# A TensorE-bound transformer step: the low parts of the attention keys on both halves of the partitions

## The chip, the cores and the metric

One core of a Trainium2 chip. The metric is the device time of one execution in microseconds (us); less is better.

## The reference

One inference step of a two-layer backbone, for 128 context tokens and 512 latent tokens, 1024 features, all in float32. Each layer: modulation, one input projection for four mixers (attention, spatial gating, retention, pooling), an output projection with residual and layer norm, and a gated convolutional feed-forward part. The change lies in the attention. It has two key heads (kv) with two query heads each (g), 64 features a head. Context queries see the context keys; the queries of a latent block of 128 see their own block, its neighbours within a window, and 128 cached keys. The two kinds share one softmax, with a sink logit beside them:

```python
s_loc = jnp.einsum("bnqkgd,bnjkd->bnkgqj", qb, kw).astype(F32) * scale
s_loc = jnp.where(valid[None, :, None, None], s_loc, NEG_INF)
s_ctx = jnp.einsum("bnqkgd,bjkd->bnkgqj", qb, ck).astype(F32) * scale
p = softmax_with_sink(jnp.concatenate([s_loc, s_ctx], axis=-1), sink).astype(v.dtype)
```

## The kernel before

Five token tiles of 128 (t = 0 is the context, 1 to 4 the latent blocks) run through both layers; weights stream from DRAM. A float32 product is made of rounded parts: an operand is split into a high part (float32r) and a low part, the rest, and high x high, high x low and low x high are summed in PSUM. For weights, ScalarE makes the high part (L245) and VectorE the low part by a subtraction (L246). The projections (fm_mms, L547 to L549, and tm_mm, L819 to L821) take these three products for each of eight row blocks of 128; a unit of 128 output features goes first over the tokens 0 to 383 (384 columns), then over 384 to 639 (256 columns).

The order of work is the order of the program's text: each engine runs its instructions in that order. `mixers` writes projections in line and weaves "lanes" between them: after each half projection `tick` runs one stage of every open lane. The attention blocks are such lanes; t = 1, 3, 0 run in one, t = 2, 4 in a second. GpSimd's affine steps of the layer before (`affine`, L503 and L504) and the retention setup (L661) are woven in by the same ticks.

The keys are 64 features a head, so head 0 lies on partitions 0 to 63 and head 1 on 64 to 127. `key_split` (L573 to L579) makes, for each head, a high part that ScalarE writes to both halves of the partitions (L578), and a low part that VectorE writes in place (L579), one tile for both heads. It runs twice a layer: on the cached keys in `attn_setup2` (128 columns, tile ckh) and on the projected, rotated keys in `mixers` (640 columns, tiles kh and kl, L1104 and L1105). `query_split` (L582 to L589) builds, for a block, queries with the high part on the head's own half (L587, ScalarE) and the low part on the other half (L588, VectorE). So one 128-row product of such a query tile with the doubled high keys sums high x high and low x high. A second product, of 64 rows, adds high x low. That is the pair in `attn_block`:

```python
T.matmul(o, z[:, h, :], kh[kv][:, cols], start=True, stop=False)
T.matmul(o, z[r0:r0 + HD, h, :], kl[r0:r0 + HD, cols], start=False, stop=True,
         tile_position=(r0, 0))
```

A block makes two stages of scores, one for each key head, each with both of its query heads; a stage is called a group below. Blocks 1 and 4 have two key blocks (256 columns) and the cached keys (128 columns), blocks 2 and 3 three key blocks (384) and the cached keys, block 0 only its own 128. Then VectorE adds the mask and takes the maximum (L766; L763 for block 0), ScalarE takes the exponential (L780), VectorE scales (L785), TensorE transposes the probabilities (L794), they are copied to SBUF (L798, L800), and TensorE multiplies with the values (L809).

Work tiles of up to 664 columns come from one pool of 25 buffers (`unit`): keys, split keys, queries, probabilities, weights' helpers. In `mixers` the split of the 640 keys stands behind the last key projection; the first query split of block 1 follows it after one more half projection (384 columns) and the copies of it.

Of the kernel before, what the change touches and what calls it, by code (L numbers as in the profile page):

```python
# [8 lines left out]
F32 = mybir.dt.float32  # L9
F32R = mybir.dt.float32r  # L10
# [4 lines left out]
P = 128  # L15
D = 1024
KD = D // P
# [72 lines left out]
def kernel(  # L90
# [38 lines left out]

    # ---- persistent tiles  # L130
    ident = one.tile([P, P], F32, name="ident")
# [18 lines left out]

    # ---- weight stream: stages in the order of their use, split ahead of it
    class Cols:
# [36 lines left out]
    class AdaFirst:  # L189
        """128 rows of the adaLN columns that the first projection waits for, used as they come"""  # L190

# [19 lines left out]
    class AdaPair:  # L211
        """a sixth of the columns and two steps for later use, in a unit's place; each step has rows of its own"""
        n = 1
# [35 lines left out]
    class Stream:  # L249
# [20 lines left out]
        def advance(self, limit=99):  # L270
            """emit splits, in stream order, while there is room for them"""
            while self.there and limit > 0 and self.live < NW // 2:
                st = self.there[0]
                self.count += not isinstance(st, AdaPair)
                eng = G if self.pool_share and self.count % self.pool_share == 0 else V
                got = st.fetch() if isinstance(st, AdaPair) else split(*st.view(self.u_split), eng)
                self.ready.append((st, got))
                self.live += 1
                limit -= 1
                self.u_split += 1  # L280
                if self.u_split == st.n:
                    self.there.pop(0)
                    self.u_split = 0
                    if not isinstance(st, AdaPair):
                        self.dma()
# [6 lines left out]
        def take(self):  # L292
            """the next unit of a projection; adaLN products before it are made on the way"""
            st, w = self.head()
            while isinstance(st, AdaPair):
                st.step(w)
                self.free()
                st, w = self.head()
            return w
# [6 lines left out]

    # ---- adaLN: rows of products in PSUM, then feature-major columns and gate rows
    class Ada:
# [31 lines left out]
    def ada_finish(a, ss):  # L340
        """columns of the features, or rows of a gate"""
        f = folds[len(ss) - 1]
        if ss[0] in (2, 5):
            pg = bank(name="adaG")
            T.matmul(pg[0:4, :], f, row, start=True, stop=True)
            gr = unit([P, 512], name="grow")
            S.activation(out=gr[0:4, :], in_=pg[0:4, :], func=AF.Copy)
            for j in range(2):
                side(out=a.scratch[ss[0] // 3, :, j * 512:(j + 1) * 512], in_=gr[2 * j:2 * j + 2, :])
            return  # L350
        n = 4 * len(ss)
        pt = bank(4 * n, name="adaT")
        for q in range(4):
            T.matmul(pt[:, q * n:(q + 1) * n], row[:, q * P:(q + 1) * P], f, start=True, stop=True)
        ptv = pt.rearrange("p (q j c) -> p q j c", q=4, c=2)
        for i, s in enumerate(ss):
            for j in range(2):
                V.tensor_copy(out=a.modT[:, s if s < 2 else s - 1, 4 * j:4 * j + 4, :], in_=ptv[:, :, 2 * i + j, :])
# [8 lines left out]

    # ---- per-layer small parameters, feature major
    def params(l, dma):
# [25 lines left out]
    def mods(a, prm_ln, which):  # L395
        """scale and bias columns [P, KD, 2] of the modulated activation"""
        sh, sc = a.modT[:, 2 * which], a.modT[:, 2 * which + 1]
# [17 lines left out]

    # ---- residual stream: alpha * x in token-major halves, kept in DRAM between uses
    xs = {}
# [51 lines left out]
    def norm_out(t, lnwb, dst):  # L469
        """the first half on VectorE, the second on ScalarE and GpSimd (and VectorE in the end)"""  # L470
        lw, lb = lnwb
# [34 lines left out]

    # ---- normalized token-major tile -> modulated, split, feature-major h
    def to_h(t, sb):
# [24 lines left out]

    # ---- feature-major projection of one 128-column unit onto tokens lo:hi
    GA, GB = (0, SPLIT_COL), (SPLIT_COL, W)

    def fm_mms(us, lo, hi, lag=0, mid=None):
        """several units side by side, each lag steps behind the one before"""
        pss = [bank(hi - lo, name="fm") for _ in us]
# [14 lines left out]

    # ================= mixers =================
    class Mix:
# [16 lines left out]
    def key_split(k, kh, kl):  # L573
        """keys of both heads: the high part of each on both halves of the partitions, the low parts in place"""
        for kv in range(2):
            r = slice(kv * HD, kv * HD + HD)
            for j in range(2):
                S.activation(out=kh[kv][j * HD:j * HD + HD, :], in_=k[r, :], func=AF.Copy)  # L578
            V.tensor_tensor(out=kl[r, :], in0=k[r, :], in1=kh[kv].bitcast(F32)[r, :], op=ALU.subtract)  # L579

    def query_split(m, c0):
        """queries of each head with the low part on the other half of the partitions"""  # L582
        z = unit([P, 4, P], name="qs").bitcast(F32R)
        for kv in range(2):
            r, o = slice(kv * HD, kv * HD + HD), slice(HD - kv * HD, P - kv * HD)
            q, zz = y8[r, 0:2, c0:c0 + P], z[:, 2 * kv:2 * kv + 2, :]
            S.activation(out=zz[r], in_=q, func=AF.Copy)  # L587
            V.tensor_tensor(out=zz[o], in0=q, in1=zz.bitcast(F32)[r], op=ALU.subtract)  # L588
        return z  # L589

    def attn_setup2(m):
        pt = bank(P, name="ckT")
        T.transpose(pt, m.ck, ident)
        u = unit([P, 3, P], name="ckh").bitcast(F32R)
        m.ckh, m.ckl = [u[:, 0, :], u[:, 1, :]], u[:, 2, :]
        key_split(pt, m.ckh, m.ckl)
# [7 lines left out]
    def decays():  # L604
        """log decays of every layer"""
        n = DEPTH * 8
        dec = small(n, "dec")
        side(out=dec, in_=ret_decay.rearrange("l a h -> (l a h)").partition_broadcast(P))
        # log_sigmoid(x) = min(x, 0) - 2 atanh(t / (2 + t)), t = exp(-|x|)
        ab = small(n, "ab")  # L610
# [22 lines left out]
    def states():  # L633
        """initial latent states"""
        for l in range(DEPTH):
# [3 lines left out]
    def centre():  # L639
        """over the value dimension"""  # L640
        n = DEPTH * 4
# [58 lines left out]

    # ---- attention
    SWAP = [(i + 16) % 32 for i in range(32)]
# [23 lines left out]
    def attn_block(m, t, first=False):  # L726
# [16 lines left out]
        for kv in range(2):  # L743
            r0 = kv * HD
            for g in range(2):
# [3 lines left out]
                while i < nb:  # L749
                    kind, bt = blocks[i]  # L750
                    w = 1
                    while kind == "k" and i + w < nb and blocks[i + w] == ("k", bt + w):
# [4 lines left out]
                    T.matmul(o, z[:, h, :], kh[kv][:, cols], start=True, stop=False)  # L757
                    T.matmul(o, z[r0:r0 + HD, h, :], kl[r0:r0 + HD, cols], start=False, stop=True,  # L758
                             tile_position=(r0, 0))
                    i += w  # L760
# [51 lines left out]

    # ---- token-major values
    def tm_mm(t, units):
# [40 lines left out]

    # ---- spatial gating: s = ws v + bs, feature major
    def sgu(m):
# [15 lines left out]

    # ---- retention
    def ret_step(m, d, t, kv, s1=None):
# [8 lines left out]
    def ret_states(m, l):  # L884
        """k^T v of every chunk and the states that enter the chunks"""
        kvp = {}
# [99 lines left out]

    # ---- multiscale pooling
    def pool_in(ps_a, ps_b):
# [44 lines left out]

    # ---- lanes: chains of stages that are woven between the projections
    lanes, late = [], []
# [21 lines left out]
    def mixers(l, m, prm, mid=None, then=None):  # L1057
# [45 lines left out]
        m.k = raws[2]  # L1103
        m.kh, m.kl = [unit([P, W], name="kh").bitcast(F32R) for _ in range(2)], unit([P, W], name="kl").bitcast(F32R)  # L1104
        key_split(m.k, m.kh, m.kl)  # L1105
# [96 lines left out]

    # ---- FFN depthwise conv
    def conv_a(cwT, f, ps):
# [22 lines left out]

    # ================= the stream of weights =================
    def wout_chunk(l, k, h):
# [41 lines left out]

    # ================= program =================
    def x_in(t):
# [16 lines left out]
    def h_first(segs, alone=0):  # L1290
        """modulated, split h from the feature-major x in y8"""
        lo, hi = segs[0][1], segs[-1][2]
# [57 lines left out]
    for l in range(DEPTH):  # L1350
# [4 lines left out]

        # output projection, residual, layer norm
        xd = drm.tile([NT, P, D], F32, tag="xd", name=nm("xd"))
# [38 lines left out]

        # gated conv FFN
        act, outs, queue = [], {}, []
# [25 lines left out]
        for i, (br, f) in enumerate(order):  # L1424
# [7 lines left out]
            while len(queue) > (4 if i < 5 else 2):  # L1432
                finish_b(queue.pop(0))
        # the last groups leave the first columns of hh and hl to the products that follow
        EARLY = 4
# [129 lines left out]
```

## Time and profile before

| | |
|---|---|
| median of three runs | 1594.93 us (1594.81 to 1595.16) |
| span of the profiled execution | 1593.2 us |
| TensorE matmul busy | 1558.6 us, 98% of the span |
| VectorE, ScalarE, GpSimd busy | 953.3, 617.9, 420.9 us |
| mean granted TensorE clock | 0.992 of full speed |

The profiled execution has no time of its own beside its span; the span, from the first to the last instruction, is 1.7 us under the median of the runs, and what lies around it is taken as the same before and after. In the profile PE is TensorE, PEld its weight load, DVE VectorE, ACT ScalarE, POOL GpSimd, SP SyncE; L758 is line 758 of the kernel. Matmuls overlap: the distance from one start to the next says what a matmul costs, its own duration does not.

### The profile page before, as it was taken

Reading aid. Unit: us, or ns where it says so; the run is one execution under the profiler, and the core shown is the slowest. Engines: PE = TensorE matmul, PEld = TensorE weight load, DVE = VectorE, ACT = ScalarE, POOL = GpSimd, SP = SyncE. Lnnn points to the kernel's source line nnn. Section 1 sums busy time; section 2 is a strip of 40 time slices with the busy share of each in tenths; the row PEclk is TensorE's granted clock in tenths of the full one; section 3 lists DMA queues with packets and bytes.
Section 4 is the critical chain, followed back from the end, with each engine's and each line's share of the span. In section 5 each row is a group of like instructions: output and inputs, shape, how many; then the busy total and the mean of one; then the engine's idle time right before and its main releaser. Section 6 shows DMA issues by size and latency. Waiting matters only on the chain.

```text
span 1593.2 us, 24481 instructions
## 1 busy us (share of the span) xinstructions
PE 1558.6 (98%) x9708; PEld 1360.9 (85%) x9708; DVE 953.3 (60%) x1856; ACT 617.9 (39%) x994; POOL 420.9 (26%) x486
## 2 busy tenths in 40 slices
PE   5999999999999999999998999999999999999997
PEld 1987878899999999988788888687999999997885
DVE  3755256686555655745577653567865666665456
ACT  2634354243333333433345344533543333343331
POOL 2400267154100101211127212742541101111104
PEclk9999999999999999999999999999999999999999
DMA  9533435234443434233315323151242122224311
GB/s 332 167 126 114 148 102 171 81 114 166 159 136 130 149 120 156 95 127 119 99 46 192 111 97 106 55 199 53 94 131 81 54 79 80 80 80 139 116 49 67
DMA packets 117791, 187.99 MB, mean 118 GB/s; under 512 B 11492, under 2 KB 77854, under 8 KB 117677
## 3 DMA queue, kind: packets, MB, share of 16 engines
q1 hardware_dynamic: 109517, 163.03, 30.2%
q0 software_dynamic: 8160, 23.40, 4.7%
q8 instruction: 76, 1.25, 0.3%
q14 instruction: 38, 0.31, 0.1%
HBM read 175.35 MB, written 11.04 MB: 117 GB/s over the span
## 4 chain that ended last, share of the span: by engine, by line
PE 88%; DVE 4%; POOL 3%; DMA 2%; issue 1%; ACT 1%; SPq 0%; POOLq 0%; ACTq 0%; DVEq 0%
PE fm L547 17%; PE fm L549 17%; PE fm L548 17%; PE dn L1471 6%; PE dn L1470 6%; PE dn L1469 6%; PE ada L233 2%; PE wo L1379 2%; PE wo L1381 2%; PE wo L1380 2%; PE sc L758 1%; DMA st<-in_w_ada_dram 1%; PE sc L757 1%; PE tm L819 1%; PE PT L794 1%
## 5 line engine op out<-in xcount | busy, mean ns | idle before, releaser
L547 PE MATMUL fm<-hh,wh 128*128 128x256 f32 (+1 forms) x1920 | 601.4, 313 | 1.6 <-ACT hh L1299 1.6
L549 PE MATMUL fm<-hl,wh 128*128 128x256 f32 (+1 forms) x1920 | 594.9, 310 | 3.2 <-DVE hl L1304 2.3
L548 PE MATMUL fm<-hh,wl 128*128 128x256 f32 (+1 forms) x1920 | 594.4, 310 | 0.0
L547 PEld LDWEIGHTS fm<-hh,wh 128*128 128x128 f32 x1920 | 363.5, 189 | 30.6 <-ACT cv L1220 11.7
L246 DVE TENSOR_TENSOR wl<-st,wh 128x1024 fp32r<-128x1024 f32 x186 | 280.4, 1515 | 180.3 <-ACT wh L245 178.3
L549 PEld LDWEIGHTS fm<-hl,wh 128*128 128x128 f32 x1920 | 362.9, 189 | 5.1 <-DVE hl L1304 3.3
L548 PEld LDWEIGHTS fm<-hh,wl 128*128 128x128 f32 x1920 | 363.3, 189 | 0.1
L245 ACT ACTIVATE wh<-st 128x1024 fp32r<-128x1024 f32 x188 | 196.3, 1053 | 215.7 <-PE dn L1470 141.9
L1210 DVE SCALAR_TENSOR_TENSOR cv<-fm,cwT,cv 128x127 f32<-128x127 f32 x352 | 122.0, 408 | 110.4 <-ACT cv L1207 110.4
L1471 PE MATMUL dn<-wh,hl 128*128 128x512 f32 x440 | 174.6, 397 | 0.3 <-DVE hl L1406 0.2
L1470 PE MATMUL dn<-wl,hh 128*128 128x512 f32 x440 | 174.1, 396 | 0.0
L1469 PE MATMUL dn<-wh,hh 128*128 128x512 f32 x440 | 173.4, 394 | 0.0
L1207 ACT ACTIVATE cv<-fm,cwT 128x384 f32<-128x384 f32 x88 | 58.9, 673 | 203.5 <-PE fm L549 188.0
L1419 POOL TENSOR_TENSOR act<-cv,cv 128x640 f32<-128x640 f32 x28 | 46.7, 1669 | 300.1 <-DVE cv L1225 232.5
L1220 ACT ACTIVATE cv<-fm,cwT 128x255 f32<-128x255 f32 x88 | 49.6, 563 | 176.5 <-PE fm L549 176.5
L1470 PEld LDWEIGHTS dn<-wl,hh 128*128 128x128 f32 x440 | 82.6, 188 | 20.4
L1471 PEld LDWEIGHTS dn<-wh,hl 128*128 128x128 f32 x440 | 82.6, 188 | 20.4 <-DVE hl L1406 1.1
L1469 PEld LDWEIGHTS dn<-wh,hh 128*128 128x128 f32 x440 | 82.6, 188 | 19.9
L1419 POOL TENSOR_TENSOR y<-cv,cv 128x640 f32<-128x640 f32 x16 | 26.9, 1678 | 182.7 <-DVE cv L1225 182.7
L1221 DVE SCALAR_TENSOR_TENSOR cv<-fm,cwT,bnd 128x1 f32<-128x1 f32 x88 | 19.1, 217 | 89.7 <-ACT cv L1220 89.6
L1379 PE MATMUL wo<-wh,hh 128*128 128x512 f32 x160 | 64.6, 404 | 0.0
L450 POOL TENSOR_TENSOR r<-ve,mhalf 128x1 f32<-128x1 f32 x20 | 16.5, 826 | 178.6 <-DVE neg L456 178.3
(290 smaller groups left out, 2081.5 us busy)
## 6 DMA issues: line engine op xcount, KB each, us to landing
st<-in_ffn_up_dram SPq DMA_DIRECT2D x44, 1024.0 KB
wa<-in_w_ada_dram SPq DMA_DIRECT2D x80, 512.0 KB
st<-in_ffn_down_dram SPq DMA_DIRECT2D x88, 256.0 KB
st<-in_w_in_dram SPq DMA_DIRECT2D x20, 1024.0 KB
st<-in_w_ada_dram SPq DMA_DIRECT2D x16, 512.0 KB
xd<-xr SPq DMA_DIRECT2D x30, 256.0 KB
xr<-xd POOLq DMA_DIRECT2D x30, 256.0 KB, 5.8
st<-in_w_out_dram SPq DMA_DIRECT2D x24, 256.0 KB
```

The lines of the kernel that those rows point to most:

```text
L245: S.activation(out=oh, in_=view, func=AF.Copy)
L246: eng.tensor_tensor(out=ol, in0=view, in1=of, op=ALU.subtract)
L547: T.matmul(ps, wh[:, k, :], hh[:, k, lo:hi], start=(k == 0), stop=False)
L548: T.matmul(ps, wl[:, k, :], hh[:, k, lo:hi], start=False, stop=False)
L549: T.matmul(ps, wh[:, k, :], hl[:, k, lo:hi], start=False, stop=(k == KD - 1))
L1207: S.activation(out=o[:, 0:n], in_=ps, func=AF.Identity, scale=cwT[:, 1, f:f + 1], bias=cwT[:, 3, f:f + 1])
L1210: V.scalar_tensor_tensor(out=o[:, a + d:b - 1 + d], in0=ps[:, a + 1 - d:b - d], scalar=cwT[:, tap, f:f + 1], in1=o[:, a + d:b - 1 + d], op ...
L1379: T.matmul(ps, hh[:, k, c0:c0 + P], wh[:, k % 2, :], start=(k == 0), stop=False)
L1419: G.tensor_tensor(out=dst, in0=a, in1=g, op=ALU.mult)
L1469: T.matmul(ps, hh[:, s_, c0:c0 + P], wh[:, k % 2, :], start=(k == 0), stop=False)
L1470: T.matmul(ps, hh[:, s_, c0:c0 + P], wl[:, k % 2, :], start=False, stop=False)
L1471: T.matmul(ps, hl[:, s_, c0:c0 + P], wh[:, k % 2, :], start=False, stop=(k == KF - 1))
```

## The change

The low part of each key head gets a tile of its own and is written to both halves of the partitions, as the high part is. The second score product then takes the whole query tile, with 128 rows, and so also adds low x low. `key_split` issues four subtractions instead of two. The cached keys' low parts take one more quarter of their work tile, the projected keys' one more work tile. Comments and docstrings are left out as well, which shifts the line numbers.

```diff
     def key_split(k, kh, kl):
...
         for kv in range(2):
             r = slice(kv * HD, kv * HD + HD)
             for j in range(2):
                 S.activation(out=kh[kv][j * HD:j * HD + HD, :], in_=k[r, :], func=AF.Copy)
-            V.tensor_tensor(out=kl[r, :], in0=k[r, :], in1=kh[kv].bitcast(F32)[r, :], op=ALU.subtract)
+            for j in range(2):
+                V.tensor_tensor(out=kl[kv][j * HD:j * HD + HD, :], in0=k[r, :], in1=kh[kv].bitcast(F32)[r, :],
+                                op=ALU.subtract)
...
-        u = unit([P, 3, P], name="ckh").bitcast(F32R)
-        m.ckh, m.ckl = [u[:, 0, :], u[:, 1, :]], u[:, 2, :]
+        u = unit([P, 4, P], name="ckh").bitcast(F32R)
+        m.ckh, m.ckl = [u[:, 0, :], u[:, 1, :]], [u[:, 2, :], u[:, 3, :]]
         key_split(pt, m.ckh, m.ckl)
...
-            r0 = kv * HD
...
                     T.matmul(o, z[:, h, :], kh[kv][:, cols], start=True, stop=False)
-                    T.matmul(o, z[r0:r0 + HD, h, :], kl[r0:r0 + HD, cols], start=False, stop=True,
-                             tile_position=(r0, 0))
+                    T.matmul(o, z[:, h, :], kl[kv][:, cols], start=False, stop=True)
...
-        m.kh, m.kl = [unit([P, W], name="kh").bitcast(F32R) for _ in range(2)], unit([P, W], name="kl").bitcast(F32R)
+        m.kh, m.kl = [[unit([P, W], name=n).bitcast(F32R) for _ in range(2)] for n in ("kh", "kl")]
         key_split(m.k, m.kh, m.kl)
```

## Rows read from the trace of the kernel before

**Rows 1.** The page: its first line, and its chain of waits by engine.

```profile
span 1593.2 us, 24481 instructions
...
PE 88%; DVE 4%; POOL 3%; DMA 2%; issue 1%; ACT 1%; SPq 0%; POOLq 0%; ACTq 0%; DVEq 0%
```

**Rows 2.** Stretches: length, busy PE PEld DVE ACT POOL (count), clock, DMA share, GB/s.

```profile
80.00:180.00 100.00, 99.86 (x701) 80.51 (x700) 50.39 (x150) 39.36 (x95) 12.40 (x17) 1.00 0.38 130
867.40:872.00 4.60, 0.15 (x1) 0.00 (x1) 4.44 (x6) 2.43 (x10) 4.52 (x4) 0.88 1.01 351
872.00:881.00 9.00, 9.00 (x33) 7.64 (x33) 6.14 (x8) 2.82 (x8) 8.75 (x8) 0.50 0.45 172
```

**Rows 3.** Timeline of TensorE, layer 0: start, duration (us), line, form.

```profile
84.06 0.34 PE L548 MATMUL fm<-hh,wl 128*128 128x384 f32 x1
84.23 0.34 PE L549 MATMUL fm<-hl,wh 128*128 128x384 f32 x1
84.41 0.28 PE L757 MATMUL sc<-kh,qs 128*128 128x256 f32 x1
84.62 0.38 PE L758 MATMUL sc<-kl,qs 64*128 64x256 f32 x1
84.93 0.33 PE L757 MATMUL sc<-ckh,qs 128*128 128x128 f32 x1
...
85.44 0.38 PE L757 MATMUL sc<-kh,qs 128*128 128x256 f32 x1
...
86.92 0.28 PE L549 MATMUL fm<-hl,wh 128*128 128x256 f32 x1
...
89.38 0.28 PE L549 MATMUL fm<-hl,wh 128*128 128x256 f32 x1
```

**Rows 4.** Timeline of TensorE elsewhere: transposes of 128 rows, retention products of 64 rows.

```profile
147.40 1.03 PE L794 MATMUL PT<-ident,P 128*128 128x128 f32 x8
148.27 0.38 PE L918 MATMUL kTr<-ident,y 128*128 128x128 f32 x2
...
204.20 0.72 PE L939 MATMUL A<-qc,y 64*128 64x128 f32 x8
204.85 0.44 PE L547 MATMUL fm<-hh,wh 128*128 128x384 f32 x1
```

**Rows 5.** Stretches of the twenty score groups, TensorE alone: two of them and their sum.

```profile
95.64:98.03 2.39, 2.39 (x10) 1.00 0.69 216
...
169.85:170.77 0.92, 0.92 (x7) 1.00 0.00 0
...
sum 42.24, PE 42.24; mean PE 2.11
```

**Rows 6.** Waits of TensorE from 840 to 970 us: in all, times, longest (us).

```profile
PE sc L757 <- DVE qs L588: 4.4, 1, 4.4
```

**Rows 7.** Instructions on the cached keys' split: count, duration ns (least/median/most), first and last start.

```profile
L579 DVE TENSOR_TENSOR ckh<-ckT,ckh x4: 276/288/295, 60.3 to 846.3; 64x128 fp32r<-64x128 f32 x4
```

**Rows 8.** Timeline of VectorE in layer 1, key and query split.

```profile
865.61 3.72 DVE L579 TENSOR_TENSOR kl<-k,kh 64x640 fp32r<-64x640 f32 x2
...
870.96 2.40 DVE L588 TENSOR_TENSOR qs<-y,qs 64x256 fp32r<-64x256 f32 x2
```

**Rows 9.** Timeline of GpSimd beside it.

```profile
868.72 1.73 POOL L504 TENSOR_TENSOR xr<-xr,lnb 128x512 f32<-128x512 f32 x1
...
879.81 1.28 POOL L504 TENSOR_TENSOR xr<-xr,lnb 128x512 f32<-128x512 f32 x1
```

**Rows 10.** Timeline of VectorE in layer 0, key and query split.

```profile
78.40 1.66 DVE L579 TENSOR_TENSOR kl<-k,kh 64x640 fp32r<-64x640 f32 x2
...
80.65 0.87 DVE L588 TENSOR_TENSOR qs<-y,qs 64x256 fp32r<-64x256 f32 x2
```

**Rows 11.** Timelines of VectorE and TensorE in layer 1, block 1's probabilities.

```profile
890.73 1.41 DVE L785 TENSOR_SCALAR P<-P,su 128x384 f32<-128x384 f32 x4
...
892.55 0.82 PE L794 MATMUL PT<-ident,P 128*128 128x128 f32 x6
```

## The prediction, made before the changed kernel was run

> **What bounds the kernel now.** I read the page first. Its chain of waits is 88% TensorE [rows 1], so the time is a queue of matmuls, and the question for any edit is what it does to the distance from one matmul's start to the next. Then the table of stretches [rows 2]: in layer 0's mixers, 80 to 180 us, TensorE is busy 99.86 of 100 us, so there every nanosecond between two starts is a nanosecond of the end. Layer 1's mixers hold one exception, 867.4 to 872 us, where TensorE does nothing and VectorE is busy 4.44 of 4.60 us. Only there does work of another engine set the end.
>
> Then the timeline of TensorE around the first score products [rows 3]. In a projection, 128 rows after 128 rows, a product of 384 columns starts 0.175 us after the one before (84.06 to 84.41, two steps), and one of 256 columns 0.117 us after (21 steps from 86.92 to 89.38). The score pair goes another way. From L757 (128 rows) to the first L758 (64 rows) it is 0.21 us, from there to the next L757 0.31, and from the 128-column L757 at 84.93 to the L757 at 85.44, two steps, 0.51, or 0.255 each. From 128 to 256 columns the step grows by 0.055 us, as it does in the projections from 256 to 384. So the surcharge is a constant, about 0.2 us a step: one part is the weight load that now starts with its matmul instead of under the one before, the other a pause of about 0.09 (0.21 against 0.117) at each change of row count. That it is the change and not the 64 rows, the transposes and the retention products tell [rows 4]: eight 128-column transposes of 128 rows take 0.87 us to the next start, 0.109 each, and eight 64-row products in a row (L939) take 0.65, 0.081 each, though their rows alternate between the halves.
>
> All twenty groups of score products together are 42.24 us from their first start to the next instruction's [rows 5]; four kinds make them up: eight groups with 256 columns (four pairs each), eight with 384, four with 128 alone (two pairs).
>
> **The change part by part.**
>
> *The second product gets 128 rows.* 144 products remain, with the same columns; I price them by the projection's steps. A 256-column group becomes 4 x 0.117 + 4 x 0.109 = 0.90 us, a 384-column one 4 x 0.175 + 4 x 0.109 = 1.14, a 128-column one 4 x 0.109 = 0.44. One of the 256-column groups, at 872 us, runs at the lower clock (0.50, 1.2 GHz, [rows 2]) and I double it to 1.8. Sum: 7 x 0.90 + 1.8 + 8 x 1.14 + 4 x 0.44 = 19.0, a gain of 23.2 us. What stays: after six groups an instruction in a column tiling follows, and four groups follow transposes; I leave each its 0.09 pause, 0.9 in all. **Gain on TensorE: 22.3 us.** The unknown is the 128-column step, which the trace shows for no such product outside the pairs. From above it is the 256-column step, 0.117 (0.6 us less gain over 80 such products); from below the stream alone, 0.117 less the 0.055 us that 128 columns cost, 0.062 (3.8 us more). I take the transposes' 0.109, since they load weights of the same 128 x 128 shape.
>
> *Four more subtractions per layer on VectorE.* Two are of cache keys, 0.29 us each [rows 7], at 60 and 846 us, under projections; the rotary work behind them waits for the projection's copy anyway. Two are of the 640 keys, and here the layers differ.
>
> Layer 0: two took 1.66 us at 78.40, so two more end the second query operation of the block, which ended at 81.52, at about 83.2, plus at most 0.6 of the cache keys [rows 10]. TensorE asks for it at 84.41 [rows 3]. Cost nothing; the cover is the 384-column projection before the scores, and without it 1.7 to 2.3 us would show.
>
> Layer 1: nothing covers it. TensorE's one long wait of its mixers is L757 on the query split, 4.4 us [rows 6], and the query split stands behind the key subtractions on VectorE's queue [rows 8]. There two took 3.72 us, 1.86 each instead of 0.83, since GpSimd's affine steps run beside them [rows 9]. Two more, between the same GpSimd steps, which go on to 880 us: **3.7 us later**. Bounds: 1.7 (as undisturbed in layer 0, [rows 10]) and 5.1 (each behind a whole GpSimd step of 1.73 us and then its own 0.83). I take the value of the two that stand just ahead. Queued behind: the decay scale, a projection copy, both query operations, then the weight split for the value products; they shift together with TensorE, which waits for the first query operation.
>
> *The clock.* After this wait the clock is 0.50 for 9.0 us [rows 2]. A longer wait ends at the same level. But if the low clock again lasts 9 us from the restart, the faster scores let the second group (8 products) fall inside: 0.9 us more. Bounds: 0, and 1.8 if another 1.8 us of work falls in.
>
> *The softmax chain.* In block 1 of each layer TensorE's probability transposes come at 892.55; the second probability tile that they need is scaled by about 891.5 [rows 11]. One score group lies between the exponentials' release and those transposes, so TensorE comes 1.27 us sooner, at 891.28, and now waits 0.2 us. Twice: 0.4. Other blocks have no score group in that stretch or over 1 us to spare.
>
> *One more buffer.* The second low part takes one of the 25 work buffers from the key split to the last score product; counted in program order, the kernel before uses 24 or 25 at its peak, in blocks 2 and 4. A few softmax tiles will take a buffer whose reader is only just done. From below 0 (the reader is TensorE in the same stage), from above one set of transposes, 1.03 us [rows 4], per layer. I take 0, as the waiting engines, ScalarE and VectorE, idle there.
>
> **Sum:** 22.3 - 3.7 - 0.9 - 0.4 = 17.3 us. The profiled execution's span is 1593.2, so 1575.9. The median of the runs is 1.7 above that span: **1577.6 us**.
>
> **The rivals.**
>
> *The weight load stays exposed.* The pause goes, but each product still begins with its own load. Then a step is the load (0.109, from the transposes) plus its stream (0.107, 0.160, 0.053): groups of 1.51, 1.72 and 0.65 us, doubled once, 29.9 in all, a gain of 12.3; less 3.7, 0.4 and the 0.9 left: 7.3, or 1587.6. Against it: the projections load 128-row weights under 128-row products at 0.117 a step [rows 3]. For it: nothing but that score products reuse one query tile. The Trainium skill, "TensorE: Matmul & The Clock Gate", Part 3, says under "What overlaps and what doesn't" that a weight load overlaps a running matmul only where the row groups differ; by that rule this rival would be the result, since all row groups are now equal. The projections' rows speak against the rule here. 8%.
>
> *The softmax takes over.* The softmax runs over VectorE and ScalarE at their own pace while TensorE's share of it shrinks, so TensorE could wait at the probability steps instead. Blocks 1 to 4 have three such steps each (two sets of transposes, one output product), 24 in both layers; with 0.5 us at half of them 6 us go: 1583.6. For it: one step that will be just late [rows 11]. Against it: projections lie between all of these steps, and TensorE waits almost nowhere in 80 to 180 us [rows 2]. 12%.
>
> *The surcharge is not the row change (slower).* If short pairs into one bank cost 0.2 us whatever their rows, TensorE gains nothing, and layer 1 pays 3.7 us of VectorE: 1594.9 + 3.7 = 1598.6. The point from which this decides is a gain of under 26 ns a product (3.7 over 144). Against it: the transposes, the L939 rows [rows 4], and that the first L757 after a projection starts without any surcharge [rows 3]. 3%.
>
> **How the numbers follow.** Forecast 75%, softmax 12%, exposed load 8%, slower 3%, something unseen 2%. The forecast's own bounds: 3.8 (128-column step) and 2.0 (subtractions) to the good, 0.6 (128-column step), 0.9 (clock), 1.4 (subtractions) and 2.1 (buffer, both layers) to the bad: 1572 to 1582.6. The low end is drawn in to 1573, since both good bounds would have to hold, and the high end reaches to 1584.5, over the softmax case: what is left out is the exposed load, the slower case and a tail. What a measurement of this kernel can tell from no change is about 0.2%, 3.2 us. Faster than that: forecast, softmax, exposed load, less a tail, 93%; within: 4%; slower 3%.
>
> **What would show it.** Right: L758 in the form 128 x 128, score groups of about 0.9, 1.1 and 0.45 us, PE steps of 0.11 between L757 and L758; four key subtractions before the first query split in layer 1 and TensorE's wait there at about 8 us; no wait at that place in layer 0. Wrong: steps of 0.16 to 0.22 (exposed load), 0.25 to 0.31 (no effect), or new waits of TensorE on probability tiles in layer 0. The prediction fails most easily in layer 1, where the wait and the low clock depend on how GpSimd and VectorE take turns.

## The result, and the profile after

The changed kernel takes 1576.02 us (median of 4 runs, 1575.2 to 1576.42). The kernel before took 1595.05 us beside it (4 runs, 1594.81 to 1595.33). The ratio is 0.988, with a 95% interval of 0.9868 to 0.9892: faster by 19.0 us, where 17.3 were forecast. The median lies 1.6 us under the predicted 1577.6 and inside the range.

The page of the changed kernel: its first line, the busy times, and the chain of waits by engine.

```profile
span 1573.4 us, 24493 instructions
...
PE 1535.4 (98%) x9708; PEld 1353.3 (86%) x9708; DVE 962.5 (61%) x1864; ACT 618.0 (39%) x994; POOL 423.3 (27%) x486
...
PE 88%; DVE 4%; POOL 3%; DMA 2%; issue 1%; ACT 1%; SPq 0%; POOLq 0%; ACTq 0%; DVEq 0%
```

The chain is what it was [rows 1]: TensorE still sets the time, and its matmuls are as many as before (9708), only closer together. The span is 19.8 us shorter (1593.2 before). The stretches of the twenty score groups, TensorE alone (length, busy, clock, DMA share, GB/s), five of them and the sum:

```profile
84.08:84.95 0.87, 0.87 (x10) 1.00 1.02 410
...
92.75:93.85 1.10, 1.10 (x10) 1.00 0.00 0
...
158.88:159.37 0.49, 0.49 (x5) 1.00 0.00 0
864.40:866.17 1.77, 1.77 (x9) 0.50 0.66 218
...
914.74:915.75 1.01, 1.01 (x11) 1.00 0.10 24
...
sum 19.45, PE 19.45; mean PE 0.97
```

They answer to [rows 5]: 42.24 us have become 19.45, so 22.8 us are gone. The timeline of TensorE shows how, in the group that [rows 3] showed from its first score product on (start, duration, line, form):

```profile
83.91 0.34 PE L549 MATMUL fm<-hl,wh 128*128 128x384 f32 x1
84.08 0.28 PE L758 MATMUL sc<-kh,qs 128*128 128x256 f32 x1
84.20 0.28 PE L759 MATMUL sc<-kl,qs 128*128 128x256 f32 x1
84.31 0.23 PE L758 MATMUL sc<-ckh,qs 128*128 128x128 f32 x1
84.38 0.27 PE L759 MATMUL sc<-ckh,qs 128*128 128x128 f32 x1
84.49 0.33 PE L758 MATMUL sc<-kh,qs 128*128 128x256 f32 x1
84.66 0.28 PE L759 MATMUL sc<-kl,qs 128*128 128x256 f32 x1
```

Read the starts, not the durations. The two 256-column steps that open the group take 0.12 and 0.11 us, as in a projection. A 128-column step is either short (0.07 from 84.31) or 0.11 (from 84.38). The product after such a pair then holds its successor up (0.17 from 84.49 to 84.66). So three steps in a row, 84.31 to 84.66, take 0.35 us, 0.117 each.

The weight loads of these products (PEld: start, duration), one of the kernel before and three of the changed one:

```profile
84.62 0.18 PEld L758 LDWEIGHTS sc<-kl,qs 64*128 64x128 f32 x1 [0.19 <-issue]
...
84.08 0.19 PEld L759 LDWEIGHTS sc<-kl,qs 128*128 128x128 f32 x1
84.20 0.19 PEld L758 LDWEIGHTS sc<-ckh,qs 128*128 128x128 f32 x1
84.32 0.19 PEld L759 LDWEIGHTS sc<-ckh,qs 128*128 128x128 f32 x1
```

Before, the load of the 64-row product starts with its product, at 84.62 [rows 3]. After, the load for the product at 84.20 starts at 84.08, under the product ahead of it.

Layer 1 pays for it. First TensorE's longest wait between 840 and 970 us. Then, on VectorE's timeline, the four key subtractions and the query split of layer 1, and the same of layer 0.

```profile
PE sc L758 <- DVE qs L590: 8.2, 1, 8.2
```

```profile
854.27 7.32 DVE L580 TENSOR_TENSOR kl<-k,kh 64x640 fp32r<-64x640 f32 x4
...
863.23 3.49 DVE L590 TENSOR_TENSOR qs<-y,qs 64x256 fp32r<-64x256 f32 x2
...
78.14 3.31 DVE L580 TENSOR_TENSOR kl<-k,kh 64x640 fp32r<-64x640 f32 x4
...
82.01 0.87 DVE L590 TENSOR_TENSOR qs<-y,qs 64x256 fp32r<-64x256 f32 x2
```

The wait was 4.4 us [rows 6]. In layer 1 four subtractions take 7.32 us, 1.83 each; two took 3.72 [rows 8]. In layer 0 four take 3.31, 0.83 each, and the query split ends at 82.88, 1.2 us before TensorE asks for it at 84.08. The stretches (length, busy PE PEld DVE ACT POOL, clock, DMA share, GB/s):

```profile
80.00:180.00 100.00, 99.85 (x777) 87.46 (x776) 53.25 (x153) 43.16 (x101) 14.27 (x18) 1.00 0.45 151
856.20:864.40 8.20, 0.00 (x0) 0.00 (x1) 8.05 (x7) 4.66 (x14) 8.04 (x6) 0.73 0.83 307
864.40:870.10 5.70, 5.70 (x26) 5.70 (x27) 5.64 (x7) 0.53 (x2) 5.59 (x5) 0.50 0.33 115
```

Layer 0 has no new wait: 99.85 of 100 us are busy, as before [rows 2]. After the long wait, the granted clock is 0.50 (1.2 GHz) for 5.7 us, where it was so for 9.0.

One more wait is there, and hidden. These are rows of ScalarE in layer 1 (in brackets the idle time ahead, and what ended it): the first is the changed kernel, the other two the kernel before.

```profile
860.95 0.85 ACT L589 ACTIVATE qs<-y 64x256 fp32r<-64x256 f32 x2 [3.46 <-POOL Dt L663]
...
868.72 0.84 ACT L587 ACTIVATE qs<-y 64x256 fp32r<-64x256 f32 x2
871.70 0.76 ACT L718 ACTIVATE V<-vT 128x384 f32<-128x384 f32 x2 [2.14 <-POOL Dt L661]
```

In the kernel before, the copy of the values (V) waits for GpSimd's last Dt step, a part of the retention setup; the query split does not. In the changed kernel it is the query split that waits, 3.46 us. The Dt step reads a work tile of the same pool, and the key split now takes one tile more, so by the named releaser the query tile has drawn the buffer that V had drawn. It costs nothing here, since VectorE's subtractions end later still (861.59, against 860.91 for the Dt step). It will matter in e3 and e5.

The account of the 19.8 us of span, from the two traces:

| | measured | forecast |
|---|---|---|
| twenty score groups, 42.24 to 19.45 us | -22.8 | -22.3 |
| layer 1's wait, 4.45 to 8.21 us | +3.8 | +3.7 |
| the 24 projection products after it, 5.28 to 4.70 us (more of them at full clock) | -0.6 | +0.9 |
| waits at the probability transposes | 0 | +0.4 |
| start of the first score group, 84.41 to 84.08 us | -0.3 | 0 |
| sum | -19.9 | -17.3 |

The last term need not be the change's: in the eleven other runs below, that first group starts between 84.1 and 86.0 us, and in e5 and h2, one kernel run twice, at 85.31 and 84.38.

### The profile page after: what moved, and what is told of

It reads as the page before. It is cut to its first block, busy times and chain, and to the rows that moved or that the text cites. A ratio compares the mean times of both kernels' runs of the same rounds, so it can differ in the third digit from the quotient of the medians.

```text
span 1573.4 us, 24493 instructions
## 1 busy us (share of the span) xinstructions
PE 1535.4 (98%) x9708; PEld 1353.3 (86%) x9708; DVE 962.5 (61%) x1864; ACT 618.0 (39%) x994; POOL 423.3 (27%) x486
## 4 chain that ended last, share of the span: by engine, by line
PE 88%; DVE 4%; POOL 3%; DMA 2%; issue 1%; ACT 1%; SPq 0%; POOLq 0%; ACTq 0%; DVEq 0%
PE fm L547 18%; PE fm L549 17%; PE fm L548 17%; PE dn L1470 6%; PE dn L1471 6%; PE dn L1469 6%; PE ada L233 2%; PE wo L1379 2%; PE wo L1381 2%; PE wo L1380 2%; DMA st<-in_w_ada_dram 1%; PE PT L794 1%; PE po L809 1%; PE tm L819 1%; PE tm L821 1%
```

## The experiments

The result leaves three questions. Is it the *alternation* of 128 and 64 rows that cost 22.8 us, or the 64 rows themselves? Is the 3.8 us wait the two subtractions and nothing else? And do the subtractions cost 1.83 us because GpSimd runs beside them, so that moving one or the other would win the time back? Where a time of before is compared, it is that of the same chip: 1595.47 us for e1 to e4, 1595.5 for e5 to e8, 1595.15 for h1 to h3.

**e1: the order alone.** The kernel before, with its 64-row products, in another order (cut from the edit).

```diff
+            for o, h, kh, kl, cols, fst, lst in jobs:
+                T.matmul(o, z[:, h, :], kh[kv][:, cols], start=fst, stop=False)
+            for o, h, kh, kl, cols, fst, lst in jobs:
+                T.matmul(o, z[r0:r0 + HD, h, :], kl[r0:r0 + HD, cols], start=False, stop=lst,
+                         tile_position=(r0, 0))
```

`jobs` holds the products of both query heads of the group. The start mark now stands only on the first product of a head; the changed kernel keeps the old marks and is as fast, so the marks are not what cost the time.

> The kernel before, with the order inside a group changed: all 128-row products of both heads first, then all 64-row products. Same 144 products, same columns, same row counts, no extra subtraction; the tiling changes twice in a group instead of at every product. Theory (the change of row count costs the pause of 0.09 us and exposes the next weight load, 0.2 us in all): groups of about 1.3 (256 columns), 1.5 (384) and 0.8 us (128), 26 to 27 us in all against 42.2, the wait before layer 1's scores stays at 4.4 us, time about 1579. Rival (the 64-row form or the short pairs cost 0.2 us whatever the order): groups stay at 42 us, time 1595.

Measured: 1576.51 us, ratio 0.9882 (0.9865 to 0.9898). TensorE's timeline of the first group in layer 0:

```profile
84.78 0.28 PE L761 MATMUL sc<-kh,qs 128*128 128x256 f32 x1
84.90 0.22 PE L761 MATMUL sc<-ckh,qs 128*128 128x128 f32 x1
84.96 0.33 PE L761 MATMUL sc<-kh,qs 128*128 128x256 f32 x1
85.12 0.22 PE L761 MATMUL sc<-ckh,qs 128*128 128x128 f32 x1
85.28 0.38 PE L763 MATMUL sc<-kl,qs 64*128 64x256 f32 x1
85.50 0.22 PE L763 MATMUL sc<-ckh,qs 64*128 64x128 f32 x1
...
85.73 0.22 PE L763 MATMUL sc<-ckh,qs 64*128 64x128 f32 x1
85.88 0.39 PE L547 MATMUL fm<-hh,wh 128*128 128x256 f32 x1
```

```profile
sum 24.01, PE 24.00; mean PE 1.20
```

The second fence is the sum of the twenty groups. Inside either run of equal rows, the steps are 0.06 to 0.17 us; only the last step ahead of a change of rows (85.12 to 85.28, 85.73 to 85.88) and the first behind it (85.28 to 85.50) are long. The same 72 products of 64 rows that stood in 42.24 us of groups now stand in 24.01. So 18.2 of the 22.8 us were the alternation, and 64 rows are not slow. The other 4.6 go with the two changes of rows that each group still has, 0.115 each over forty; a few tenths of them are the low clock, which reached the second group of layer 1 (1.35 us at a mean clock of 0.80, where the like group of layer 0 took 1.09).

**e2: the subtractions alone.** The kernel before, whose key split also writes the two low parts that the change adds, into a tile that nothing reads.

```diff
+            o = slice(HD - kv * HD, P - kv * HD)
             V.tensor_tensor(out=kl[r, :], in0=k[r, :], in1=kh[kv].bitcast(F32)[r, :], op=ALU.subtract)
+            V.tensor_tensor(out=kx[o, :], in0=k[r, :], in1=kh[kv].bitcast(F32)[r, :], op=ALU.subtract)
```

> The kernel before, with the two additional subtractions of every key split alone, written to a spare tile that nothing reads; the score products are those of before (64 rows for the second). Theory: layer 0 hides them, in layer 1 TensorE's wait on the query split grows from 4.4 to about 8.2 us, time 1595 plus 3.8, less up to 1.6 if the low clock again ends sooner: 1597 to 1599. Rival (the longer wait in the changed kernel came from TensorE arriving sooner or from the full buffers, not from the subtractions): wait 4.4 us, time 1595.

Measured: 1599.32 us, ratio 1.0025 (1.0015 to 1.0035), so +3.9 us. VectorE's timeline in layer 1, the waits of TensorE, and the stretch after the restart (length, TensorE busy, clock):

```profile
867.22 1.91 DVE L579 TENSOR_TENSOR kl<-k,kh 64x640 fp32r<-64x640 f32 x1
869.15 1.79 DVE L581 TENSOR_TENSOR kx<-k,kh 64x640 fp32r<-64x640 f32 x1
```

```profile
PE sc L759 <- DVE qs L590: 8.2, 1, 8.2
```

```profile
877.35:886.80 9.45, 9.45 (x34) 0.50 0.27 97
```

The wait of the changed kernel is there, 8.2 us, without the change on TensorE. The spare tile takes a buffer too, and ScalarE's query split waits for the Dt step here as well (3.48 us); but VectorE goes from the subtractions to the query split, 876.19, with no idle time, so they set the wait and not the buffer. The two parts add: +3.9 here and -22.8 there. The last row separates the clock too: with the old order of products and the same 8.2 us wait the low clock lasts 9.45 us, against 9.0 after a wait of 4.45 [rows 2]. So the longer wait alone does not shorten it.

**e3: zeros instead of subtractions.** Low x low isn't needed: in this kernel the other half of the low tiles holds zeros, which VectorE writes earlier, behind the cached keys' split (so low x low is left out, as in the kernel before).

```diff
-            for j in range(2):
-                V.tensor_tensor(out=kl[kv][j * HD:j * HD + HD, :], in0=k[r, :], in1=kh[kv].bitcast(F32)[r, :],
-                                op=ALU.subtract)
+            V.tensor_tensor(out=kl[kv][r, :], in0=k[r, :], in1=kh[kv].bitcast(F32)[r, :], op=ALU.subtract)
...
+            V.memset(m.ckl[kv].bitcast(F32)[o, :], 0.0)
+            V.memset(m.kl[kv].bitcast(F32)[o, :], 0.0)
```

> The changed kernel with the other half of each low-part tile set to zero by a memset (placed behind the cached keys' split, ahead of the rotary work) instead of a second subtraction; both products keep 128 rows, low x low is left out as in the kernel before. Theory: score groups as in the changed kernel, 19.4 us in all; the wait in layer 1 back to about 4.4 us, so 3.8 us less than the changed kernel: 1572.3, or 1573.9 if the low clock then lasts 9 us after the wait as it did in the kernel before. Rival (the memsets only move the work on VectorE's queue ahead of the same wait): 1576.

Measured: 1578.25 us, ratio 0.9893 (0.9878 to 0.9907). A miss: the wait is 7.1 us though only two subtractions are left. ScalarE's and VectorE's timeline before the restart at 864.28 (in brackets the idle time ahead, and what ended it):

```profile
856.68 3.70 DVE L579 TENSOR_TENSOR kl<-k,kh 64x640 fp32r<-64x640 f32 x2
...
862.76 0.85 ACT L587 ACTIVATE qs<-y 64x256 fp32r<-64x256 f32 x2 [2.87 <-POOL Dt L666]
863.21 2.44 DVE L588 TENSOR_TENSOR qs<-y,qs 64x256 fp32r<-64x256 f32 x2 [1.22 <-ACT qs L587]
```

The subtractions are done at 860.4. The query split waits for ScalarE, and ScalarE waits for GpSimd's Dt step (L666): the wait that was hidden in the changed kernel. With two subtractions fewer it is what ends last, so a part of what they saved is paid back by a buffer; e5 below has this alone, a wait of 5.7 us where the kernel before has 4.4. The rest is the rival of the expectation. The memsets stand ahead of the rotary work on VectorE and put off all that follows: the key subtractions start 0.5 us before TensorE stops (856.68 and 857.20), in e5 below 1.9 us (855.51 and 857.42). These 1.4 us are the difference between the waits of e3 and e5, 7.1 and 5.7. A second wait of TensorE comes on top in e3, 2.3 us at block 1's probability transposes (L797).

**e4: GpSimd held back.** The changed kernel, with layer 1's affine steps held while the key split runs.

```diff
-        if late:
+        if late and not held[0]:
```

> The changed kernel with GpSimd's affine steps of layer 1 held back from the third key projection until block 1's first query split is issued; they follow later, one a tick. Theory (a subtraction takes 1.83 us instead of 0.83 because GpSimd's steps take turns with it): the four subtractions shrink from 7.3 us to 3.3 to 5.3 (two retention steps of GpSimd stay there), the wait from 8.2 to 4 to 6 us, time 1572 to 1574. Rival (the subtractions are long in layer 1 for another reason, the DMA traffic there for one): wait stays 8.2 us, 1576; or the affine steps collide as much where they are put: 1576 with a short wait.

Measured: 1582.26 us, ratio 0.9917 (0.9902 to 0.9932), slower than the change. VectorE's split in layer 1, its softmax step behind it, and TensorE's waits:

```profile
855.16 3.31 DVE L580 TENSOR_TENSOR kl<-k,kh 64x640 fp32r<-64x640 f32 x4
...
877.35 0.56 DVE L766 CUSTOM_DVE_ANT_0 P<-sc,mask 128x384 f32<-128x384 f32 x1 [4.95 <-POOL xr L503]
```

```profile
PE PT L794 <- DVE P L785: 12.1, 1, 12.1
PE sc L758 <- DVE qs L590: 2.8, 2, 2.5
```

The first row answers the first half of the third question: with GpSimd idle (854.2 to 859.9 us) four subtractions take 3.31 us in layer 1 as well, and the wait falls from 8.2 to 2.5. The DMA traffic, the other suspect, does not do it alone: in the changed kernel's layer 0 four took 3.31 us at 352 GB/s (78.14 to 81.45 us), in its layer 1 7.32 at 293 GB/s (854.27 to 861.59). But the affine steps work on tiles of the same pool (`xr`, `lnb`). Held back, they are late with them, and by the second row the softmax (L766), which draws its tiles from that pool, sits idle for 4.95 us until an affine step (L503) is done. TensorE stands 12.1 us at the probability transposes instead. That the pool is the reason rests here, and in e6 to e8, on the releasers that the profile names: no run had more buffers.

**e6: GpSimd moved, not held.** The changed kernel with two affine steps earlier, the hold as in e4 but shorter, and one step more behind it.

```diff
+            late.pop(0)()
+            late.pop(0)()
             ws.advance()
             attn_setup2(m)
...
+        held[0] = l > 0
         start_b(2)
         start_b(3)
```

> The changed kernel with three of GpSimd's affine steps of layer 1 moved: two of them earlier, ahead of the first second-half projection, one a tick later; none of them runs beside the four subtractions, and none after it is later by more than a tick. Theory: subtractions of 0.83 to 1 us, the wait 2.5 to 4 us instead of 8.2 and too short for the low clock, so 5 to 8 us less than the changed kernel: 1568 to 1571; the 12.1 us wait of the run that held all of them back came from work buffers that the held steps had not released, and is gone. Rival (the affine steps cost the same wherever they stand, since VectorE and GpSimd must take turns somewhere on the way to TensorE): 1576.

Measured: 1576.92 us, ratio 0.9884 (0.9867 to 0.99), no gain on the change. TensorE's waits, and the step that caused the second:

```profile
PE PT L794 <- DVE P L785: 4.4, 1, 4.4
PE sc L758 <- DVE qs L590: 2.5, 1, 2.5
```

```profile
873.20 0.56 DVE L766 CUSTOM_DVE_ANT_0 P<-sc,mask 128x384 f32<-128x384 f32 x1 [3.32 <-POOL xr L503]
```

The wait is cut by 5.7 us and 4.4 come back, with a second stretch of low clock behind them.

**e7 and e8: the same move** on e1 and on e5 (below).

> The grouped order (kernel before, 128-row products first, then the 64-row ones, no additional subtraction or buffer) with the same three affine steps moved. Theory: groups of 24.0 us, two subtractions of 0.83 to 1.2 us, the wait 1 to 2.5 us and no low clock: 5 to 7 us less than the grouped order alone, 1569.5 to 1571.5. Rival: 1576.5.

> The zero halves by ScalarE with the same three affine steps moved. Theory: groups of 19.4 us, two undisturbed subtractions, the wait 1 to 2.5 us, no low clock: the fastest of the four, 1566 to 1568. Rival: ScalarE's two zero copies now stand ahead of the query split and end the wait instead of VectorE, wait 3 to 4 us: 1569.

Measured: e7 1579.78 us, ratio 0.9903 (0.9888 to 0.9917); e8 1577.16, 0.9888 (0.9874 to 0.9903). Both are some 3 us slower than the kernel they start from, and the same pattern shows: the query wait falls to 2.4 (e7) and 4.4 us (e8), and a wait of 3.7 and 4.5 us on the probabilities appears. In e8 VectorE's softmax (L766) waits 3.31 us for an affine step, in e7 ScalarE's value copy 7.51 us. Three kernels say the same of the move, so it isn't a version to keep.

**e5: zeros by ScalarE.** As e3, but ScalarE writes them (key times 0) in the key split, and the tiles are taken where the change takes them.

```diff
+            o = slice(HD - kv * HD, P - kv * HD)
+            S.activation(out=kl[kv][o, :], in_=k[r, :], func=AF.Copy, scale=0.0)
+            V.tensor_tensor(out=kl[kv][r, :], in0=k[r, :], in1=kh[kv].bitcast(F32)[r, :], op=ALU.subtract)
```

> The changed kernel with the other half of each low-part tile written as zero by ScalarE (key times 0) instead of by a second subtraction on VectorE; the tiles are allocated where the changed kernel allocates them, so that the order in which the 25 buffers go round is the changed kernel's. Low x low is left out, as in the kernel before. Theory: groups as in the changed kernel (19.4 us), two subtractions of 3.7 us instead of four of 7.3, TensorE's wait back to 4.4 to 5 us, 3 to 3.8 us less than the changed kernel: 1572 to 1573 (1574.5 if the low clock then lasts 9 us). What the first zero-half run showed (a wait of 7.1 us, ScalarE's query split held by GpSimd's retention step) came from the buffer that the query tile drew, and is gone. Rival (fewer subtractions don't shorten the wait, something else ends it): 7 to 8 us, 1576 to 1578.

Measured: 1573.88 us, ratio 0.9866 (0.9851 to 0.9881), the fastest. VectorE and ScalarE in layer 1, and TensorE's wait:

```profile
855.51 3.71 DVE L581 TENSOR_TENSOR kl<-k,kh 64x640 fp32r<-64x640 f32 x2
...
861.60 0.85 ACT L589 ACTIVATE qs<-y 64x256 fp32r<-64x256 f32 x2 [1.65 <-POOL Dt L663]
```

```profile
PE sc L758 <- DVE qs L590: 5.7, 1, 5.7
```

Two subtractions take 3.71 us again, as in the kernel before, but the wait is 5.7 and not 4.4: here too the query split waits for GpSimd's Dt step, as it did unseen in the changed kernel.

**h1 to h3: the three best, side by side.** The changed kernel, e5 and e1 again, unedited, five rounds on one chip.

> The changed kernel again, unedited, on the same chip as h2 and h3. Both theories: about 1576.0 us, ratio 0.988; TensorE's wait on the first query split of layer 1 at 8.2 us again.

> The changed kernel with ScalarE writing zeros into the other half of the low parts instead of VectorE's two extra subtractions (the same as e5). If the 2.1 us between e5 and the changed kernel are the shorter wait (5.7 against 8.2 us): about 1573.9 us and about 2 us under h1. If they came from another chip or another day: equal to h1 within 0.5 us.

> The kernel before with the products of a group ordered by their row count (the same as e1). If the order alone is worth as much as the change: 1576.5 us, within 1 us of h1.

Measured: h1 1575.74 us, ratio 0.9877 (0.9863 to 0.9892); h2 1573.31, 0.9862 (0.9847 to 0.9876); h3 1576.91, 0.9882 (0.9865 to 0.9898). The medians differ as in the first runs: e5's version is 2.4 us under the change, and its wait is again 5.7 us against 8.2 (2.5 less). The intervals of the ratios overlap; the runs themselves do not (1572.61 to 1573.95 against 1575.42 to 1576.25). e1's version stands 1.2 us above h1, with runs that overlap (1575.48 to 1577.16). Its account gives 0.9: 4.6 us more in the groups, and 3.7 us less wait (4.5 against 8.2).

## Why the prediction was right

**The gain on TensorE: right, 22.3 forecast, 22.8 measured.** e1 shows the reason that the prediction gave: the surcharge belongs to the change of row count, since the same products in another order lose most of it. Of its two parts, the loads show one: before, a load starts with its product, after, under the one ahead. Its sizes held too. A 256-column group takes 0.87 to 1.01 us (0.90 forecast), a 384-column one 1.10 to 1.20 (1.14), a 128-column one 0.40 to 0.50 (0.44), the group at the low clock 1.77 (1.8). The unknown 128-column step had been bounded by 0.062 and 0.117; the traces show both ends in turn, and the mean is close to the 0.109 that the transposes gave. Of the 0.9 us left for other neighbours some 0.5 showed (19.45 against the priced 19.0).

**The exposed weight load: excluded.** It wanted groups of 1.5 and 1.7 us. The loads of equal rows lie under the products before them, at 0.12 us a 256-column step, so the rule of the Trainium skill ("TensorE: Matmul & The Clock Gate", Part 3, "What overlaps and what doesn't") does not hold for these rows, as the projections had already said.

**The subtractions: right.** 3.7 us forecast, 3.8 measured, and 3.9 alone in e2. That GpSimd's steps double their time was read from two rows; e4 shows it, 3.31 us for four without those steps against 7.32 with them. Layer 0's cover held: 99.85 of 100 us busy.

**The clock: the step that failed.** "If the low clock again lasts 9 us from the restart" was taken as 0.9 us of loss; it lasted 5.7, and the 24 projection products behind the first group gained 0.6. A length seen once had been taken for a fixed one, and counted from the restart, though the clock falls within the wait: by the mean clocks 0.73 and 0.88 of the two waits (a mix of 1.00 and 0.50), some 4.4 us of the low clock lay in the longer wait and 1.1 in the shorter one [rows 2], and in all it lasted 10.1 us in both. What sets that length stays open: see the last section.

**The softmax chain: a small miss.** The 0.4 us at two transposes did not show in the first profile; in h1 0.2 us did, in one place, and in h2 0.6. These two terms (1.5 and 0.4) are most of the 2.5 us by which the span came out under the forecast 1575.9. The median is only 1.6 under its own: the profiled execution was the fastest of the four (1575.2 us, 1.8 above its span), so the median stands 2.6 above the span and not 1.7.

**The buffer: right at nothing, by luck in part.** As the prediction said, ScalarE had idle time for it; but the buffer wait it meets is 3.46 us long, at the query split and not at the softmax, and it is free only because the subtractions end later. e3 and e5 uncover it. And e4 and e6 to e8, which hold affine steps back, show new waits of 3.7 to 12.1 us. The bound of 1.03 us a layer, one set of transposes, was far too low for that.

## What to carry to other kernels

Count the changes of row count in TensorE's order before counting rows: here each cost about 0.16 us where they alternate (22.8 us over 144 products), more than a whole 256-column product at 0.117, and grouping the products by row count (e1, a change of order with no work added) brought nearly the same time as widening them. When work is added to an engine to spare another, look which stage has no cover for it, and give it to the engine that is idle there (ScalarE in e5, for 2.4 us). And before a step is moved, ask which buffers it releases and who draws them next: in four kernels here (e4, e6 to e8) the wait that was removed came back, by the releasers named, at the next user of the pool, and in the change itself one tile more moved a wait onto the query split, where a longer one hid it.

## What was not expected of the hardware

**How long the low clock lasts.** After the wait in layer 1 the granted clock was at 1.2 GHz for 9.0 us in the kernel before and 9.45 in e2 (rows alternating), 7.7 in e1 and 5.0 in h3 (the same kernel, another execution), 5.7 and 5.5 in the changed kernel, 5.6 and 4.5 in e5 and h2. The length of the wait does not order these (8.2 us of wait stand with 9.45 and with 5.7), and one and the same kernel differs by 2.7 us. Adding the part that falls into the wait does not make them equal: it gives 10.1 us for the kernel before and the changed one, but 13.6 in e2 (mean clock 0.75 in 8.2 us of wait) and 6.7 in h3 (0.81 in 4.5 us). The two executions with alternating rows are the longest, but why was not tried. Short waits were not safe either: after one of 2.5 us the clock stayed full in e4, and in e6 it fell to 0.50 about one microsecond after the restart, for some 3 us.

**A second product right behind its twin.** With the same 128-row query tile as the one before it and only 128 columns, a product starts 0.06 to 0.07 us after it; the next two starts are then 0.11 and 0.17 us apart. The three together take what three 256-column steps take, 0.35 us, so the short step is no gain. The weight loads set the pace there: in the changed kernel's group they start every 0.11 to 0.12 us, whatever the columns (84.08, 84.20, 84.32, and on to 84.43, 84.54, 84.66).
